# Four product blocks by token halves ahead of a norm, three behind it, and split weights in the common ring

## The chip, the cores and the metric

The kernel runs on one core of a Trainium2 chip. The metric is the device time of one execution in microseconds (us). The median of three runs of the kernel before is 2490.06 us (2487.38 to 2491.95).

## What is computed

Two models one after the other on a sequence of 512 tokens of width 1024, all in float32. The first is one layer with three branches (a forgetting attention, a complex diagonal state-space model, an attention on a memory of 256 rows) and a last norm; the second is two layers (a full attention and three dilated ones) whose norms are shifted and scaled by a projection of a condition c. What the change touches are the products with weights and the norms between them, cut here to:

```python
y = x * rsqrt(mean(x * x, -1) + 1e-6) * g          # rms(x, g), in front of every product below
x = x + merged @ w_out; x = rms(x, g_final)         # end of the first model
for l in range(2):                                  # the second model
    h = rms(x, g_mix[l]) * (1 + sc1) + sh1
    parts = split(h @ w_in[l]); ...                 # attentions on parts give "merged"
    x = x + gt1 * (merged @ w_out[l])
    h2 = rms(x, g_mlp[l]) * (1 + sc2) + sh2
    x = x + gt2 * (square(relu(h2 @ w_ff1[l])) @ w_ff2[l])
```

## The kernel before

**Layout.** Activations lie transposed: eight tiles x[0] to x[7] of 128 features by 512 tokens. A block is a PSUM tile of 128 output features by 512 tokens, the sum over eight tiles of the input.

**Products.** A float32 product is made of three products of fp32r numbers: high times high, low times high, high times low (`mm3`, L108 to L110). So a block of depth 8 takes 24 matmuls of 512 columns. Weights are split on the chip: `fetch` loads a strip of 128x1024 (tag wr), `split` makes the high part with a cast on ACT (tag wh, L88) and the low part with a subtract (tag wl, L90), strips alternating between DVE and POOL. wr, wh and wl have three buffers each in a pool of their own, and `get` splits the strip that it hands out and the two behind it. All other tiles of 128x512 come from one ring of NU = 73.

**Norm.** Squares of x are summed over the eight tiles on ACT and DVE into sacc (`sq_acc`, L174, L175). `rstd` sums sacc over partitions on PE (`sumcols`, L181), DVE makes nv (L199), POOL the power nr (L201), PE spreads nr over the partitions (`bcast`, L188). `hi` then makes hu = x times gain times nr on DVE (L551) and the high half h on ACT (L213, or L215 with a shift); `lo` makes the low half l on DVE (L221, L223). In the norm of block 1 the same steps stand at L1069 and around it, with two norms in one.

**Around a norm.** `tail` emits the last two blocks of the product ahead of a norm by halves of 256 tokens: both blocks for the first half, then both for the second. `head` emits the norm (stat is `rstd`, then hi and lo, each by halves) and the first two blocks (HN = 2; three for "u" in block 1) behind it, by halves too: h against wh and wl (L584, L585), then l against wh (L588). This stands at: the start (norm of x, then "u"), the end of block 1 (then "qa" of layer 0), "out" then "f1" in each of the two layers, and the last "f2" of layer 0 (then "qa" of layer 1). The feed-forward runs in four quarters c, each with f1 and f2; every f2 has a tail.

**Query and key stages.** `qk_stages` norms the heads of a q or k block: squares on ACT (L611), their sums on PE (L617), DVE, POOL and DVE again (a value cut in three parts, L258 to L262, into mcq), PE (L268), ACT (qr, L277), PE (L634), DVE (L635), then the copies of `put`. They run as generators, a stage behind each later block (`run_lag`); `flush` runs what is left. `d_proj(1)` is the projection of one group of the dilated attention in `layer`, and a flush stands at its end. mcm is the same kind of value for the merging of heads.

**Order.** Instructions are emitted in program order with priorities; the framework's scheduler then sets each engine's queue by its own estimate of times, so the rows of a queue can differ from the text. `tick` feeds background work (the condition's projection `ada_gen`, on DVE with loads on SP) between blocks; `drain` finishes it.

## Time and profile before

| what | value |
|---|---|
| median of three runs | 2490.06 us (2487.38 to 2491.95) |
| the profiled execution | 2493.03 us, of which its span 2491.2 us |
| PE, DVE, ACT, POOL busy | 94%, 62%, 42%, 34% of the span |
| mean granted TensorE clock | 0.973 |

A row of a timeline shows the start in us, how long it lasted, the engine, the line, the operation, output<-inputs, the tile and a count; in brackets, the idle time of the engine just before and what ended it. Matmuls overlap in the pipeline, so the pace of PE is the distance from one start to the next, not the duration shown. The granted clock is a share of full speed; 1.00 is 2.4 GHz and 0.5 is 1.2 GHz.

### The profile page before, as it was taken

Reading aid. Unit: us, or ns where it says so; the run is one execution under the profiler, and the core shown is the slowest. Engines: PE = TensorE matmul, PEld = TensorE weight load, DVE = VectorE, ACT = ScalarE, POOL = GpSimd, SP = SyncE. Lnnn points to the kernel's source line nnn. Section 1 sums busy time; section 2 is a strip of 40 time slices with the busy share of each in tenths; the row PEclk is TensorE's granted clock in tenths of the full one; section 3 lists DMA queues with packets and bytes.
Section 4 is the critical chain, followed back from the end, with each engine's and each line's share of the span. In section 5 each row is a group of like instructions: output and inputs, shape, how many; then the busy total and the mean of one; then the engine's idle time right before and its main releaser. Section 6 shows DMA issues by size and latency. Waiting matters only on the chain.

```text
span 2491.2 us, 32131 instructions
## 1 busy us (share of the span) xinstructions
PE 2343.6 (94%) x12162; PEld 1956.8 (79%) x12162; DVE 1543.0 (62%) x2394; ACT 1036.4 (42%) x1639; POOL 840.3 (34%) x637
## 2 busy tenths in 40 slices
PE   7998889988999889998999999998999999999999
PEld 6876667877888767787887888887778887888888
DVE  7666776666898787557378674257875646522222
ACT  5435443443323336543434324334465343423432
POOL 2445446544222463126122122216431622212221
PEclk9999889999999899999999999999999999999999
DMA  5211112322775421122136562232211313232232
GB/s 186 90 48 53 51 60 85 119 68 68 251 259 203 136 89 51 34 69 84 60 119 252 192 224 102 93 119 91 66 54 57 93 56 123 77 101 93 93 102 85
DMA packets 105611, 265.29 MB, mean 106 GB/s; under 512 B 13664, under 2 KB 23408, under 8 KB 105456
## 3 DMA queue, kind: packets, MB, share of 16 engines
q1 hardware_dynamic: 104304, 261.47, 31.4%
q8 instruction: 96, 1.57, 0.3%
q10 hardware_dynamic: 1152, 1.77, 0.2%
q14 instruction: 59, 0.48, 0.1%
HBM read 244.69 MB, written 9.44 MB: 102 GB/s over the span
## 4 chain that ended last, share of the span: by engine, by line
PE 47%; DVE 7%; issue 3%; ACT 2%; DMA 2%; POOL 2%; SPq 1%; DVEq 0%; POOLq 0%; ACTq 0%
PE pmm L108 13%; PE pmm L109 13%; PE pmm L110 13%; PE ps L311 3%; DMA adw<-in_wada 1%; PE ppv L400 1%; PE ppv L402 1%; PE ppv L401 1%; POOL wl L90 1%; DMA xs<-xg 1%; DVE unm L336 1%; DVE xs L624 0%; ACT qk L650 0%; DVE adacc L505 0%; DVE rs L430 0%
## 5 line engine op out<-in xcount | busy, mean ns | idle before, releaser
L108 PE MATMUL pmm<-h,wh 128*128 128x512 f32 (+1 forms) x2232 | 853.6, 384 | 14.7 <-DVE gt L1072 4.1
L90 POOL TENSOR_TENSOR wl<-wr,wh 128x1024 fp32r<-128x1024 f32 (+1 forms) x173 | 423.2, 2446 | 1290.7 <-ACT wh L88 1067.1
L110 PE MATMUL pmm<-h,wl 128*128 128x512 f32 (+1 forms) x2232 | 851.6, 382 | 3.4 <-POOL wl L90 2.8
L109 PE MATMUL pmm<-l,wh 128*128 128x512 f32 (+1 forms) x2232 | 853.0, 382 | 0.0
L88 ACT CAST wh<-wr 128x1024 fp32r<-128x1024 f32 (+1 forms) x346 | 358.2, 1036 | 906.9 <-PE pmm L109 705.0
L108 PEld LDWEIGHTS pmm<-h,wh 128*128 128x128 f32 x2232 | 423.5, 190 | 96.6 <-ACT h L213 5.3
L110 PEld LDWEIGHTS pmm<-h,wl 128*128 128x128 f32 x2232 | 423.6, 190 | 81.5 <-POOL wl L90 3.8
L109 PEld LDWEIGHTS pmm<-l,wh 128*128 128x128 f32 x2232 | 423.8, 190 | 75.4 <-DVE l L221 1.3
L90 DVE TENSOR_TENSOR wl<-wr,wh 128x1024 fp32r<-128x1024 f32 (+1 forms) x173 | 225.5, 1303 | 164.9 <-ACT wh L88 161.9
L960 DVE SCALAR_TENSOR_TENSOR x<-pmm,ada,x 128x512 f32<-128x512 f32 (+1 forms) x100 | 64.2, 642 | 214.0 <-PE pmm L110 213.7
L383 DVE TENSOR_TENSOR pl<-pe,ph 128x512 fp32r<-128x512 f32 (+4 forms) x168 | 121.1, 731 | 117.9 <-ACT ph L381 107.2
L311 PE MATMUL ps<-qk,qk 128*128 128x512 f32 (+4 forms) x416 | 143.9, 380 | 21.8 <-POOL qk L671 9.1
L505 DVE SCALAR_TENSOR_TENSOR adacc<-adw,cact,adacc 128x512 f32<-128x512 f32 x168 | 156.2, 939 | 3.2 <-DMA adw<-in_wada 0.2
L221 DVE TENSOR_TENSOR l<-r,h 128x512 fp32r<-128x512 f32 x64 | 59.3, 928 | 121.5 <-ACT h L213 121.3
L311 PEld LDWEIGHTS ps<-qk,qk 128*128 128x128 f32 x416 | 81.2, 200 | 43.9 <-POOL qk L671 11.3
L379 ACT ACTIVATE pe<-ps 128x512 f32<-128x512 f32 (+4 forms) x168 | 84.4, 503 | 66.4 <-PE ps L311 48.0
L108 PE MATMUL pmm<-yh,wh 128*128 128x512 f32 (+1 forms) x244 | 93.3, 385 | 4.1 <-ACT yh L1402 2.6
L110 PE MATMUL pmm<-yh,wl 128*128 128x512 f32 (+1 forms) x244 | 92.5, 381 | 0.6 <-POOL wl L90 0.6
L381 ACT CAST ph<-pe 128x512 fp32r<-128x512 f32 (+4 forms) x168 | 88.8, 529 | 8.3 <-POOL y L431 2.1
L109 PE MATMUL pmm<-yl,wh 128*128 128x512 f32 (+1 forms) x244 | 92.2, 379 | 0.0
L402 PE MATMUL ppv<-pl,v 128*128 128x512 f32 (+2 forms) x216 | 78.0, 361 | 14.2 <-DVE pl L383 14.1
L336 DVE TENSOR_REDUCE unm<-ps 128x1 f32<-128x512 f32 (+2 forms) x112 | 64.7, 596 | 31.3 <-PE ps L311 30.8
(366 smaller groups left out, 3895.2 us busy)
## 6 DMA issues: line engine op xcount, KB each, us to landing
wr<-in_w SPq DMA_DIRECT2D x324, 512.0 KB
adw<-in_wada SPq DMA_DIRECT2D x192, 256.0 KB
xs<-xg SPq DMA_DIRECT2D x136, 64.0 KB
wr<-in_w SPq DMA_DIRECT2D x22, 384.0 KB
xd<-x SPq DMA_DIRECT2D x16, 256.0 KB
x<-xd SPq DMA_DIRECT2D x16, 256.0 KB
x<-in_x SPq DMA_DIRECT2D x16, 128.0 KB
x<-in_x SPq DMA_DIRECT2D x8, 256.0 KB
```

Source lines behind the costliest of these rows:

```text
L88: self.nc.scalar.copy(h[:, 0:n], r[:, 0:n])
L90: eng.tensor_tensor(out=l[:, 0:n], in0=r[:, 0:n], in1=f32(h)[:, 0:n], op=ALU.subtract)
L108: mm(out, wh, ah, start=start, stop=False)
L109: mm(out, wh, al, start=False, stop=False)
L110: mm(out, wl, ah, start=False, stop=stop)
L311: mm(outs[i] if len(r.shape) == 2 else outs[i].rearrange("p (r i) -> p r i", r=r.shape[1]), w, r, start=first and i == 0, stop=last and i ...
L336: nc.vector.tensor_reduce(out=nm, in_=pts[0], axis=AX.X, op=ALU.max, negate=True)
L379: nc.scalar.activation(out=e[:, w], in_=pt[:, w], func=AF.Exp)
L381: nc.scalar.copy(ph[:, w], e[:, w])
L383: nc.vector.tensor_tensor(out=pl[:, w], in0=e[:, w], in1=f32(ph)[:, w], op=ALU.subtract)
L402: mm(self.cut(pv, c), vh, lo, start=False, stop=z)
L505: nc.vector.scalar_tensor_tensor(out=acc, in0=w, scalar=cc, in1=acc, op0=ALU.mult, op1=ALU.add)
```

## The change

1. **Splits.** A strip is split in pieces of 512 columns. The two or more wh and wl tiles come from the common ring, which grows from 73 to 85; the pool of weights keeps wr alone. A cast no longer waits for one of three wh buffers; a dependency that only the scheduler sees puts it behind the last matmul emitted so far.
2. **Tails.** Ahead of a norm the tail has four blocks (NT = 4; the fourth in another PSUM bank, tag "s") in place of two. The norm is built before the tail; stat(0) is emitted behind the first block of the second half, hi(0) behind the second one. f2 of the first three quarters has no tail any more: eight full blocks. The last f2 of the kernel keeps two blocks.
3. **Heads.** Three blocks (HN = 3) in place of two, except "u", which has two in place of three. Where a tail began the norm, the head leaves stat(0) and hi(0) out.
4. **Order of the rest.** The condition's projection is drained before the tail in block 1 and in the last f2 of layer 0.
5. **hu.** Both halves of a norm share eight hu tiles; before, each half had eight of its own.

The diff, cut:

```diff
-    NU = 73
-    NW = 3, 3, 3
+    AFTER = mybir.DependencyInfo(mybir.DependencyClass.NoSync, mybir.DependencyReason.SCHED_ONLY)
+    NU = 85
+    NW = 3, 3
@@ split
-        h = self.t(self.wp, [128, 1024], F32R, "wh", self.NW[1])
-        l = self.t(self.wp, [128, 1024], F32R, "wl", self.NW[2])
-        self.nc.scalar.copy(h[:, 0:n], r[:, 0:n])
         eng = self.nc.gpsimd if i % self.WP == self.WP - 1 else self.nc.vector
-        eng.tensor_tensor(out=l[:, 0:n], in0=r[:, 0:n], in1=f32(h)[:, 0:n], op=ALU.subtract)
-        self.hl[i] = (h, l)
+        self.hl[i] = []
+        for c in range(0, n, T):
+            m = min(T, n - c)
+            h, l = self.u(F32R, "wh"), self.u(F32R, "wl")
+            ins = self.nc.scalar.copy(h[:, 0:m], r[:, c:c + m])
+            if self.pe is not None:
+                self.tc.add_manual_dep(ins.ins, self.pe, self.AFTER, reason="weights")
+            eng.tensor_tensor(out=l[:, 0:m], in0=r[:, c:c + m], in1=f32(h)[:, 0:m], op=ALU.subtract)
+            self.hl[i].append((h, l))
@@ mm3 (fm, tm and head keep the name of their last matmul in the same way)
-        mm(out, wl, ah, start=False, stop=stop)
+        self.pe = mm(out, wl, ah, start=False, stop=stop).ins.name
@@ norm, hi(hf), and the same in the norm of block 1
-                u = self.u(name="hu")[:, 0:256]
+                if hf == 0:
+                    us.append(self.u(name="hu"))
+                u = self.half(us[j], hf)
@@ head
-    def head(self, names, h, posts, norm, view, byw=False):
+    def head(self, names, h, posts, norm, view, byw=False, begun=False):
...
-        stat(0)
-        hi(0)
+        if not begun:
+            stat(0)
+            hi(0)
@@ tail
-    def tail(self, name, act, posts):
+    def tail(self, name, act, posts, norm=None):
         ws = [self.get(name, 8) for _ in posts]
-        pms = [self.p("mm") for _ in posts]
+        pms = [self.p("mm" if i < 3 else "s") for i in range(len(posts))]
...
                 self.tick(2.6)
+                if norm is not None and hf == 1 and i < 2:
+                    norm[i](0)
@@ constants
-    HN = 2
+    HN = 3
+    NT = 4
@@ layer, out (block 1's out alike, with the background drained ahead of the tail)
-        for s in range(3):
-            for f in self.strip(f"out{l}", xm, 8, [res(2 * s + b, 16, True) for b in range(2)]):
-                f()
-        self.tail(f"out{l}", xm, [res(6 + b, 16, True) for b in range(2)])
+        nt = self.NT
+        for f in self.strip(f"out{l}", xm, 8, [res(j, 16, True) for j in range(8 - nt)]):
+            f()
         h = self.new_h()
         norm = self.norm(x, mod[:, 8:16], ada[:, 24:32], h)
+        self.tail(f"out{l}", xm, [res(j, 16, True) for j in range(8 - nt, 8)], norm)
@@ layer, feed-forward
-            for s in range(3):
-                for f in self.strip(f"f2{l}", F, 8, [res(2 * s + b, 40, sq) for b in range(2)]):
-                    f()
-            self.tail(f"f2{l}", F, [res(6 + b, 40, sq) for b in range(2)])
+            nt = 0 if c < 3 else 2 if out is not None else self.NT
+            for f in self.strip(f"f2{l}", F, 8, [res(j, 40, sq) for j in range(8 - nt)]):
+                f()
+            if c == 3:
+                norm = None
+                if out is None:
+                    del h
+                    self.drain(g)
+                    h = self.new_h()
+                    self.mod[l + 1] = self.mod_cols(l + 1)
+                    norm = self.norm(x, self.mod[l + 1][:, 0:8], self.ada[l + 1][:, 0:8], h)
+                self.tail(f"f2{l}", F, [res(j, 40, sq) for j in range(8 - nt, 8)], norm)
@@ block 1, behind the first norm
-        self.head(["u"] * 3, h, [upost(j) for j in range(3)],
+        self.head(["u"] * 2, h, [upost(j) for j in range(2)],
                   norm, self.half, True)
```

How it moves the queues, at three places. Lines of the changed kernel are nine higher for the same statement (L117 to L119 are L108 to L110, L190 is L181, L197 is L188, L593 is L584, L93 is L88, L662 is L650, L222 is L213).

PE, between "out" and "f1" of layer 0, before (xh and xl are the input of out, ps the small sums, ppv and pmm the two blocks of the head):

```order
L109 MATMUL pmm_11667<-xl_11426,wh_11620 128x256
L110 MATMUL pmm_11667<-xh_11425,wl_11621 128x256
L181 MATMUL ps_11798<-c_2_67,sacc_11477 128x1 x2
L188 MATMUL ps_11805<-c_2_67,nr_11803 128x128 x2
L181 MATMUL ps_11844<-c_2_67,sacc_11477 128x1 x2
L584 MATMUL ppv_11796<-h_11780,wh_11654 128x256
L585 MATMUL ppv_11796<-h_11780,wl_11655 128x256
```

PE there now, around the sums of the first half:

```order
L119 MATMUL pmm_12335<-xh_12028,wl_12240 128x256
L117 MATMUL pmm_12335<-xh_12041,wh_12239 128x256
L190 MATMUL ps_12478<-c_2_67,sacc_12159 128x1 x2
L118 MATMUL pmm_12335<-xl_12042,wh_12239 128x256
L119 MATMUL pmm_12335<-xh_12041,wl_12240 128x256
```

and around the spreading of nr:

```order
L117 MATMUL pmm_12336<-xh_12064,wh_12298 128x256
L118 MATMUL pmm_12336<-xl_12065,wh_12298 128x256
L197 MATMUL ps_12485<-c_2_67,nr_12483 128x128 x2
L119 MATMUL pmm_12336<-xh_12064,wl_12299 128x256
L117 MATMUL pmm_12336<-xh_12077,wh_12298 128x256
```

Before, sums, spreading and the first product of the head stand directly behind one another, behind the last product of out. Now 28 matmuls of 256 columns of out stand between the sums and the spreading, and 34 between the spreading and the first product of the head. The other norm of layer 0's end and the one of layer 1 have the same pattern; at the end of block 1 there are nine matmuls between sums and spreading.

ACT, at the start, before (sq are the squares of x, h the high half of the first norm):

```order
L174 ACTIVATE sq_167<-x_114 128x256
L88 CAST wh_235<-wr_131 128x1024
L174 ACTIVATE sq_170<-x_115 128x256
L174 ACTIVATE sq_173<-x_116 128x256
L174 ACTIVATE sq_176<-x_117 128x256
L174 ACTIVATE sq_179<-x_118 128x256
L88 CAST wh_241<-wr_239 128x1024
L213 CAST h_182<-hu_211 128x256
```

and now:

```order
L222 CAST h_188<-hu_228 128x256
L222 CAST h_186<-hu_222 128x256
L222 CAST h_187<-hu_225 128x256
L222 CAST h_188<-hu_228 128x256
L222 CAST h_189<-hu_231 128x256
L93 CAST wh_234<-wr_131 128x512
L222 CAST h_189<-hu_231 128x256
L93 CAST wh_238<-wr_131 128x512
L93 CAST wh_244<-wr_242 128x512
```

The first cast of a weight stood between the squares of x; now it stands behind 15 of the 16 casts of h. On PE, sums and spreading of both halves now stand ahead of the first product.

ACT, at the flush at the end of `d_proj(1)` of layer 0, before (qk are the copies of `put`, qr the rows of the last stage, wh_10623 and wh_10803 weights of the products that follow):

```order
L277 CAST qr_10476<-ps_10471 128x512
L277 CAST qr_10499<-ps_10494 128x512
L650 CAST qk_10488<-xg_10334 64x512
L650 CAST qk_10491<-xg_10334 64x512
L88 CAST wh_10623<-wr_10347 128x1024
L88 CAST wh_10803<-wr_10555 128x1024
L650 CAST qk_10504<-xg_10414 64x512
L650 CAST qk_10510<-xg_10414 64x512
```

and now:

```order
L662 CAST qk_11114<-xg_10956 64x512
L662 CAST qk_11117<-xg_10956 64x512
L286 CAST qr_11125<-ps_11120 128x512
L662 CAST qk_11130<-xg_11040 64x512
L662 CAST qk_11136<-xg_11040 64x512
L93 CAST wh_11177<-wr_10827 128x512
L93 CAST wh_11181<-wr_10827 128x512
```

The casts of the next weights now stand behind all copies of the flush (wh_11177 and wh_11181 are the second strip of the products of v, pmm_11267 and pmm_11388). On PE, 23 products of 256 columns are left between the last sums of squares (L617) and the last spreading of mcq (L268) of this flush; the products with wh_11177 come behind the first scores (L311).

## Rows read from the trace of the kernel before

**Rows 1.** The page, busy time and instructions of each engine.

```profile
PE 2343.6 (94%) x12162; PEld 1956.8 (79%) x12162; DVE 1543.0 (62%) x2394; ACT 1036.4 (42%) x1639; POOL 840.3 (34%) x637
```

**Rows 2.** Waits of PE: who ended them; us in total, times, longest.

```profile
PE ps L268 <- DVE mcq L262: 20.2, 9, 3.8
...
PE ps L188 <- POOL nr L201: 10.4, 5, 2.7
```

**Rows 3.** PE by stretches: length, busy (instructions), granted clock, DMA share, GB/s.

```profile
1290.00:1320.00 30.00, 26.78 (x181) 0.89 0.11 36
...
2122.00:2152.00 30.00, 26.79 (x179) 0.89 0.11 36
800.00:842.00 42.00, 36.13 (x235) 0.84 0.26 85
...
1320.00:1340.00 20.00, 17.48 (x77) 1.00 0.89 322
```

**Rows 4.** Timeline of PE, from out to f1 of layer 0.

```profile
1294.94 0.50 PE L181 MATMUL ps<-c,sacc 128*128 128x1 f32 x4
1298.19 1.23 PE L188 MATMUL ps<-c,nr 128*128 128x128 f32 x4 [2.74 <-POOL nr L201]
...
1300.53 0.58 PE L584 MATMUL ppv<-h,wh 128*128 128x256 f32 x1 [0.47 <-ACT h L215]
...
1304.41 0.28 PE L585 MATMUL pmm<-h,wl 128*128 128x256 f32 x1
1304.53 0.28 PE L584 MATMUL ppv<-h,wh 128*128 128x256 f32 x1
```

**Rows 5.** Timeline of DVE, POOL and ACT in the same place.

```profile
1293.31 2.39 POOL L90 TENSOR_TENSOR wl<-wr,wh 128x1024 fp32r<-128x1024 f32 x1 [11.78 <-ACT wh L88]
1293.58 2.40 DVE L175 TENSOR_TENSOR sacc<-sacc,sq 128x256 f32<-128x256 f32 x1 [0.83 <-ACT sq L174]
...
1296.52 1.61 POOL L201 TENSOR_TENSOR nr<-nv,mhalf 128x2 f32<-128x2 f32 x1 [0.82 <-DVE nv L199]
...
1297.50 0.41 DVE L175 TENSOR_TENSOR sacc<-sacc,sq 128x256 f32<-128x256 f32 x1
...
1299.45 0.88 DVE L551 SCALAR_TENSOR_TENSOR hu<-x,modc,ps 128x256 f32<-128x256 f32 x2 [1.54 <-PE ps L188]
1299.97 3.35 ACT L215 ACTIVATE h<-hu,ada 128x256 fp32r<-128x256 f32 x8 [3.14 <-DVE hu L551]
```

**Rows 6.** Timeline of PE, from block 1 to layer 0.

```profile
812.05 0.95 PE L181 MATMUL ps<-c,sacc 128*128 128x1 f32 x8
817.42 1.19 PE L188 MATMUL ps<-c,nr 128*128 128x128 f32 x4 [4.42 <-DVE nr L1069]
```

**Rows 7.** Timeline of ACT and PE at the start.

```profile
12.56 1.04 ACT L88 CAST wh<-wr 128x1024 fp32r<-128x1024 f32 x1 [1.90 <-DMA wr<-in_w]
...
16.70 0.58 PE L584 MATMUL ppv<-h,wh 128*128 128x256 f32 x1 [3.11 <-ACT h L213]
...
19.11 1.01 PE L181 MATMUL ps<-c,sacc 128*128 128x1 f32 x4 [1.41 <-DVE sacc L175]
```

**Rows 8.** Timeline of PE: a merging of heads, then the flush, in layer 0.

```profile
929.89 0.61 PE L268 MATMUL ps<-c,mcm 128*128 128x128 bf16 x4 [3.39 <-DVE mcq L262]
...
1146.15 1.05 PE L617 MATMUL ps<-c,sq 128*128 128x2 f32 x8 [0.44 <-ACT sq L611]
...
1156.57 0.40 PE L268 MATMUL ps<-c,mcq 128*128 128x128 bf16 x4 [3.77 <-DVE mcq L262]
...
1164.85 0.39 PE L634 MATMUL ps<-qr,c 128*128 128x512 bf16 x1
```

**Rows 9.** Casts of ACT by line and form: ns shortest/median/longest, first and last start.

```profile
L88 ACT CAST wh<-wr x346: 817/1052/1082, 12.6 to 2470.9; 128x1024 fp32r<-128x1024 f32 x162, 128x768 fp32r<-128x768 f32 x11
...
L213 ACT CAST h<-r x64: 619/621/626, 1321.5 to 2446.0; 128x512 fp32r<-128x512 f32 x64
L213 ACT CAST h<-hu x16: 399/406/408, 16.2 to 29.5; 128x256 fp32r<-128x256 f32 x16
```

More of the change, by code (lines that the diff above doesn't have):

```diff
@@ L101, in get @@
         self.iw += 1
-        n = self.strips[i][1].shape[-1]
-        return tuple(t[:, 0:n].rearrange("p (k c) -> p k c", k=kb) for t in self.hl.pop(i))
+        c = self.strips[i][1].shape[-1] // kb
+        per = T // c
+        hl = self.hl.pop(i)
+        self.hl[i] = None
+        return [tuple(t[:, c * (k % per):c * (k % per) + c] for t in hl[k // per]) for k in range(kb)]
     def mm3(self, out, wh, wl, ah, al, start=True, stop=True):
@@ L109, in mm3 @@
         mm(out, wh, al, start=False, stop=False)
-        mm(out, wl, ah, start=False, stop=stop)
+        self.pe = mm(out, wl, ah, start=False, stop=stop).ins.name
     def fm(self, out, w, c0, act, kb):
-        (wh, wl), (ah, al) = w, act
-        for k in range(kb):
-            self.mm3(out, wh[:, k, c0:c0 + 128], wl[:, k, c0:c0 + 128], ah[k], al[k], k == 0, k == kb - 1)
+        ah, al = act
+        for k, (wh, wl) in enumerate(w):
+            self.mm3(out, wh[:, c0:c0 + 128], wl[:, c0:c0 + 128], ah[k], al[k], k == 0, k == kb - 1)
     def tm(self, out, ws, act, tok, cols=slice(0, 256)):
@@ L121, in tm @@
         mm = self.nc.tensor.matmul
-        ks = [(wh[:, k, cols], wl[:, k, cols]) for wh, wl in ws for k in range(wh.shape[1])]
+        ks = [(wh[:, cols], wl[:, cols]) for w in ws for wh, wl in w]
         for k, (wh, wl) in enumerate(ks):
@@ L125, in tm @@
             mm(out, ah[k][:, tok], wl, start=False, stop=False)
-            mm(out, al[k][:, tok], wh, start=False, stop=k == len(ks) - 1)
+            self.pe = mm(out, al[k][:, tok], wh, start=False, stop=k == len(ks) - 1).ins.name
     def tick(self, us=5.2):
@@ L541, in norm @@
         sacc = self.sums["sacc"]
-        pr, hu = {}, {}
+        pr, hu, us = {}, {}, []
         def stat(hf):
@@ L582, in head @@
                 for k in range(8):
[L583 to L585 removed]
+                    for w, o in g:
+                        mm(o, w[k][0], ah[k], start=k == 0, stop=False)
+                        mm(o, w[k][1], ah[k], start=False, stop=False)
                 for k in range(8):
[L587 to L588 removed]
+                    for w, o in g:
+                        self.pe = mm(o, w[k][0], al[k], start=False, stop=k == 7).ins.name
         for pm, post in zip(pms, posts):
@@ L779, in tm_items, with layer @@
         return [lambda g=g: f(g) for g in range(4 // per)]
-    def layer(self, l, norm, view, x, out=None):
+    def layer(self, l, h, norm, view, x, out=None):
         nc = self.nc
-        ada = self.ada[l]
-        mod = self.mod_cols(l)
+        ada, mod = self.ada[l], self.mod[l]
         xd = self.xdram[l]
-        h = self.new_h()
         Y = {}
@@ L804, in layer @@
         ps = [post(cq, self.CA, self.SA, True, ("a", b)) for b in range(4)]
-        self.head([f"qa{l}"] * self.HN, h, ps[0:self.HN], norm(h, mod, ada), view)
+        self.head([f"qa{l}"] * self.HN, h, ps[0:self.HN], norm, view, begun=True)
         for j in range(8):
@@ L991, in layer @@
                 n = self.HN
-                self.head([f"f1{l}"] * n, h, [relu2] * n, norm, self.half)
+                self.head([f"f1{l}"] * n, h, [relu2] * n, norm, self.half, begun=True)
             for f in self.strip(f"f1{l}", h, 8, [relu2] * (8 - n)):
@@ L1495, in block1 @@
         self.load16()
-        self.merge(self.strip("u", h, 8, [upost(j) for j in range(3, 6)]), [])
+        self.merge(self.strip("u", h, 8, [upost(j) for j in range(2, 6)]), [])
         merged = []
@@ L1719, in res @@
             return f
-        for s in range(3):
-            for f in self.strip("out", ms, 8, [res(2 * s), res(2 * s + 1)]):
-                f()
-        self.tail("out", ms, [res(6), res(7)])
+        nt = self.NT
+        for f in self.strip("out", ms, 8, [res(j) for j in range(8 - nt)]):
+            f()
+        while self.bg:
+            self.drain(self.bg[0])
         xo = [self.u(name="x") for _ in range(8)]
@@ L1751, in hi @@
                 for j in range(8):
-                    u = self.u(name="hu")[:, 0:256]
+                    if hf == 0:
+                        us.append(self.u(name="hu"))
+                    u = self.half(us[j], hf)
                     self.stt(u, self.half(x[j], hf), self.gfm[:, j:j + 1], p2[hf], ALU.mult, ALU.mult)
@@ L1766, in s5_out @@
         self.gfm = self.t(self.base, [128, 8], F32, "gfm")
-        return xo, norm
+        h = self.new_h()
+        self.mod[0] = self.mod_cols(0)
+        norm = norm(h, self.mod[0], self.ada[0])
+        self.tail("out", ms, [res(j) for j in range(8 - nt, 8)], norm)
+        return xo, h, norm
 PERM = np.arange(T).reshape(128, 4).T.reshape(-1)
@@ L1995, in run @@
     def run(self, out):
-        x, norm = self.block1()
-        while self.bg:
-            self.drain(self.bg[0])
+        self.mod = {}
+        x, h, norm = self.block1()
         self.load2()
-        x = self.layer(0, norm, self.halfp, x)
-        self.layer(1, self.plain(x), self.half, x, out)
+        x, h, norm = self.layer(0, h, norm, self.halfp, x)
+        self.layer(1, h, norm, self.half, x, out)
 INS = ["x", "mem", "c32", "c16", "rope", "trow", "mb0", "cols", "w1024", "w768", "wada", "wfl", "s5p", "s5bc", "bfg"]
```

16 lines of the change are left out of this document (4 added, 12 removed).

## The prediction

> **What bounds the kernel.** I read the page first. PE is busy 94% of the span of 2491.2 us, DVE 62%, ACT 42%, POOL 34% [rows 1]: only what makes PE idle, or slow, can be won. That is some 148 us of idle time and what is lost at the lower clock (mean 0.973). The waits of PE show it in many small pieces: the query and key stages (mcq, 20.2 us in 9 waits) and the norms (nr, 10.4 us in 5) lead [rows 2]. So I went to the places that the change touches.
>
> The stretch of a norm comes three times in alike form, from out to f1 of both layers and from f2 of layer 0 to layer 1. In 30 us around the first and the last PE is busy 26.78 and 26.79 us, with a granted clock of 0.89 [rows 3]: 3.2 us idle, and 0.11 of 30 us is 3.3 us of lost clock, that is 6.6 us at 1.2 GHz. The timeline says why [rows 4]: the sums start at 1294.94, the spreading waits 2.74 us for nr and starts at 1298.19, the first product waits another 0.47 and starts at 1300.53. The low clock follows that idle time; idle time in smaller pieces need not bring it, as the stretch at 1320 us shows, with 2.5 us idle in 20 us and a clock of 1.00 [rows 3]. On the other engines [rows 5] the reader sees the links: an addition to sacc takes 2.40 us where the next takes 0.41, since it runs beside a weight subtract of POOL that takes 2.39; POOL's power of two columns takes 1.61; two steps of hu take 0.88, and eight casts of h 3.35.
>
> **The change, part by part.** The sum is made against the profiled execution, 2493.03 us, which is 2.97 above the median of the runs, 2490.06; the forecast is given against the median.
>
> *Three alike norms.* The lag between sums and spreading was 3.25 us (1294.94 to 1298.19) [rows 4]. Now 28 matmuls of 256 columns stand there. At the full clock these come 0.12 us apart (1304.41, 1304.53) [rows 4], so the cover is 3.4 us. From the spreading to the first product it was 2.34 us (1298.19 to 1300.53); now 34 matmuls, 4.1 us, stand there. Both are covered, the first barely. If so the idle 3.2 us goes; and of the 6.6 us at 1.2 GHz the part that was not idle, 3.4 us, did half its work and loses 1.7 us, which is also won. What is late next: the head's third block needs a weight whose low half now stands behind nv of the second half on DVE, and the sums of the second half have only 15 matmuls (1.8 us) before their spreading, against a lag of 3.25. That leaves 1.0 to 1.5 us of idle time. 3.2 + 1.7 − 1.2 is 3.7; the small sums and spreadings, which ran at the low clock and now run among products, give some 0.3 more. I take 4.0 each, **12.0** together. Bounds: 1 each if the remaining idle time still brings the low clock, 5.2 each if nothing is late.
>
> *From block 1 to layer 0.* PE is busy 36.13 of 42 us, clock 0.84 [rows 3]. The spreading waits 4.42 us, at a distance of 5.37 from the sums [rows 6]. Only nine matmuls (1.1 us) now stand between; some 3.3 us of that wait stay and may bring the low clock again, while what comes behind is covered. Bounds: 0 and 5. I take the middle, **2.5**.
>
> *The start.* The first cast of a weight began at 12.56, and the first product at 16.70 [rows 7]. Products then came at the pace of h, and after the sums at 19.11 (1.01 us) without a break, so the start was worth being full from about 20.1. Now the first cast stands behind 15 casts of h. The first of these started at 16.2 and one takes 0.41 [rows 9]; they follow hu, of which one takes 0.44 (0.88 for two) [rows 5]. The fifteenth ends at about 16.2 + 14 × 0.44 + 0.41 = 22.8, and half a strip's cast of 0.62 ends at 23.4 [rows 9]. The loss is 23.4 − 20.1 = **3.3**. Bounds: 1.8 (the sums of the second half are out of the way by then) and 5 (the low half on DVE comes later too).
>
> *Splits.* A strip's cast was 1.05 us; two pieces take 2 × 0.62 = 1.24 [rows 9]: 0.19 more for each of 346 strips, 66 us at most on ACT, which is busy 1036 of 2491 us [rows 1]. ACT's own work hides it; if ACT were the last in a stage, the price would be there in full. I put it at nothing, but for the two places named (start, flush).
>
> *Shapes of products.* The full blocks of three quarters' f2, the tails of four and the heads of three change which products run with 256 columns and which with 512: 24 more of 512 and 48 fewer of 256. 48 of 256 at 0.12 are 5.8 us, and 24 of 512 are about the same, a little less by what each matmul costs beside its columns; I take **0.3** won (bounds 0 and 0.6).
>
> *Attention.* Casts no longer wait for one of three buffers, and the order of PE shifts. A wait for mcm of 3.39 us [rows 8], alike in both layers, now has 6.6 us of products ahead of them in the order in place of 0.7: 6.8 us to be won at most. The flush that follows gives some back. Between its last sums (1146.15) and its last stage (1164.85) lay 18.7 us, with 0.44 and 3.77 us of idle time [rows 8]. Now only 23 products of 256 columns (2.8 us) stand between the last sums and the last spreading, and the next weights' casts come behind all copies: two of 0.62. I take half of the first, 3.4 won, and two such casts late in each layer, 2.4 lost: **1.0** won. Bounds: 6.8 won, 21.8 lost (the rival below).
>
> The sum: −12.0 − 2.5 + 3.3 − 0.3 − 1.0 = **−12.5**; the profiled execution would be 2480.5 us, the median 2477.6, so **2478**. The terms' own uncertainty gives 2472 to 2484.
>
> **The rivals.** *More is won.* The addition to sacc took 2.40 us beside a subtract of POOL [rows 5]; half-length subtracts would hold it up half as long, some 1.2 us, and there are other such meetings on the way to the norms and in the flush. Six places of 1.2 us are 7 us: 2471. For it speaks that row; against it that most steps of DVE are not waited for. The Trainium skill's page "SBUF — State Buffer", section "Who interferes with whom", says that a DVE instruction with two SBUF inputs contends with a GpSimd instruction that reads SBUF, and that the loser is fully blocked for the whole instruction. By that rule, halving the subtract halves the block, and the time would be this rival's; the trace agrees as far as the pair of 2.39 and 2.40 goes.
>
> *No change.* The three norms give about 1 us each, since the spreading of the second half comes too early and what idle time is left still brings the low clock, block 1's end gives nothing with its nine matmuls, and the start takes 3.3: −3 + 3.3 − 0.3 − 1 = −1, 2489. That would be a change that doesn't do what it says. For it speaks the barely covered lag (3.4 against 3.25); against it that the second wait is fully covered.
>
> *Slower: the flush.* The chain from the last sums to the last stage took 18.7 us, mostly beside products [rows 8]. If it takes as long with 2.8 us of products and some 1 us of small ones beside it, PE is idle 15 us in place of 4.2 in each of two layers: +10.8 twice, 21.6, against the forecast's 2.4 or so. The time is 2478 + 22 = 2500. It decides from about 6 us of added idle time per layer, where all else that is won is gone. For it speaks that all of the chain's copies are on DVE, ACT and POOL, whatever PE does. Against it: part of the 18.7 us was queueing behind subtracts of weights and copies that have moved away, and the waits for mcq before were no longer than 3.8 [rows 2].
>
> **How the numbers follow.** A measurement of this kernel can tell about 0.2% (5 us) from no change. Chances: forecast 0.46, more won 0.13, no change 0.23, slower 0.18. Faster by over 0.2% (under 2485) is the first two, 0.59, and a little of the third, so 0.60; no change is the rest of the third, 0.22; slower (above 2495) 0.18. The range reaches below to 2464 (more won, with the norms' upper bound of 5.2 each) and above to 2500, which leaves out half of the slower case and little else. The forecast's own range is 2472 to 2484.
>
> **What would show it.** Right: in the three norms, PE's waits for nr gone or under 1 us and the granted clock of such a stretch at 0.97 or more in place of 0.89; the first product at about 23 us at the start; waits for mcm near nothing; the flush within 2 us of before. Wrong: a clock still below 0.93 around the norms, or a wait of PE at the end of the flush of over 8 us, or new waits of PE for wl or wh of over 10 us in sum, which would mean that the splits come too late.

## The result and the profile after

The changed kernel takes 2459.40 us (median of 4 runs, 2458.20 to 2460.29) against 2490.52 us (2487.38 to 2491.95): a ratio of 0.9876, 95% interval 0.9859 to 0.9894, so 31 us faster. The forecast was 12.5 us faster, 2478 (2464 to 2500).

The page of the changed kernel answers to [rows 1] and, for the casts, to the idle time that the three buffers made (its last two rows; idle time and what ended most of it stand at the end of a row):

```profile
span 2457.6 us, 33152 instructions
...
PE 2322.2 (94%) x12138; PEld 1938.8 (79%) x12138; DVE 1538.6 (63%) x2573; ACT 1064.0 (43%) x1995; POOL 887.5 (36%) x810
...
L93 ACT CAST wh<-wr 128x512 fp32r<-128x512 f32 (+1 forms) x692 | 385.1, 610 | 136.8 <-DMA wr<-in_w 118.8
L96 DVE TENSOR_TENSOR wl<-wr,wh 128x512 fp32r<-128x512 f32 x346 | 278.8, 836 | 30.3 <-ACT wh L93 26.9
```

and the row of the kernel before for the same casts:

```profile
L88 ACT CAST wh<-wr 128x1024 fp32r<-128x1024 f32 (+1 forms) x346 | 358.2, 1036 | 906.9 <-PE pmm L109 705.0
```

PE's idle time fell from 147.6 to 135.4 us (span less busy), 12 us; its busy time fell by 21.4 us at equal work, since the mean granted clock rose from 0.973 to 0.981. Casts waited for PE before (a buffer of wh to be done with); now they wait for their load.

**A table by stage.** To see where the time goes, I laid the starts of PE's instructions of two traces beside each other at equal work: each matmul counts as what it takes at the full clock (0.227 us for 512 columns, 0.1185 for 256), and a stage is a stretch of that sum. What stands there is how much a kernel falls behind the kernel before over a stage, in us, negative where it is faster (one profiled execution of each kernel; the last stage, under 1.5 us everywhere, is only in the sum). The stages end at 61, 131, 384, 781, 864, 1283, 1342, 1405, 1642, 1696, 2113 and 2171 us of the kernel before: the start; two stretches of block 1; its attention and state-space part ("attn 1" is 131 to 384 us); the passage to layer 0; layer 0's attention; its norm; the first of its f1; the rest of the feed-forward; the norm of layer 1; and so on. A stage is good to about 2 us. The sums are up to 7 us more favourable than the medians of the runs, as the profiled execution of the kernel before, 2493.03 us, was one of its longer ones: cast_halves has −8.2 in the table and −1 by its runs.

```
kernel            start  -131  attn1  rest1  to l0  attn l0  norm   f1  ff  norm  attn l1  norm   all
changed             9.7  -5.0  -11.8    4.5    3.3    -16.0  -5.9 -2.3   0  -4.7     -0.3  -4.8 -33.7
halves_in_pool     -1.0  -0.4  -10.6    2.1   -2.3      0.1  -2.0 -0.5  -1  -3.1     -0.7  -2.1 -21.6
splits_only        12.1  -4.9   -4.9    3.8   -1.1    -11.3   1.1 -2.4  -1   3.1     -1.5   2.7  -4.7
no_overlap          9.1  -4.9  -10.1    5.0   -5.8    -10.7   0.2 -2.3  -1   2.9     -0.2   1.7 -16.5
early_split        15.3  -4.9   -5.6    6.9    2.9    -15.6  -6.2 -2.4  -1  -4.6     -0.6  -4.8 -21.0
mid_split           4.0  -5.2   -6.0    4.5    3.4    -14.9  -6.0 -2.4   0  -4.7      1.1  -4.7 -31.0
pool_halves        -1.4  -1.3  -19.4   -1.7   -1.9     -1.2  -2.8 -1.5   0  -1.8      0.6  -1.9 -34.6
dve_halves         -0.6  -0.4   -8.0    1.6    2.7     -0.9   0.0  0.6   0  -0.6     -2.4  -0.9  -8.8
cast_halves         0.6  -1.1  -12.0    2.5    1.6     -0.6   0.5  0.4   0   0.0     -0.1  -0.1  -8.2
norms_only         -0.9   0.9  -17.0   -0.1    3.5     -6.1   3.5 -2.3  -1   6.4      5.2   6.3  -2.0
before_pool_256    -1.4  -1.8  -16.6   -4.8   -4.8      1.1  -1.1 -1.2  -1  -2.4      4.5  -2.5 -32.1
pool_halves_nt3    -2.0  -0.8  -15.2   -2.6   -3.9     -2.7   1.2 -2.6  -1  -0.2     -0.5   0.9 -30.6
after_pool_256      9.6  -3.6  -11.1    3.6    2.5    -14.4  -6.1 -2.6  -1  -4.6      1.1  -4.8 -32.2
before_u2          -1.0   0.7  -18.9    0.5    1.4     -2.1   0.1 -0.5   0  -1.3     -2.2   0.1 -22.7
before_swapped      2.0  -5.7  -15.1   -5.2    4.2     -3.8  -0.5 -0.3   0  -0.3      2.1  -0.6 -23.1
after_swapped       9.1  -1.1  -11.6    0.1    1.1     -7.4  -4.0 -2.3   0  -3.4      1.3  -3.5 -22.6
no_after           10.3  -5.2  -10.6    4.4    5.3    -15.2  -6.0 -2.6   0  -4.7      0.2  -4.6 -29.4
hybrid             -0.4  -2.2  -14.8   -4.2   -3.4     10.0  -6.2 -2.3   0  -4.7     14.5  -4.8 -19.1
after_nu73          9.6  -5.0  -12.0    8.6   -1.4     13.2  -6.0 -2.3   0  -4.7     13.5  -4.5   8.1
```

The reader is to see four things in the first row: the three norms (−15.4 together), a start that loses 9.7, and two stretches of attention, −11.8 and −16.0, that the prediction did not have (it had 1.0 us won in all attention).

**The norms.** PE's timeline between out and f1 of layer 0 in the changed kernel answers to [rows 4]:

```profile
1274.22 0.50 PE L190 MATMUL ps<-c,sacc 128*128 128x1 f32 x4
1278.02 0.60 PE L197 MATMUL ps<-c,nr 128*128 128x128 f32 x4
...
1289.44 0.71 PE L197 MATMUL ps<-c,nr 128*128 128x128 f32 x4 [0.55 <-POOL nr L210]
1290.96 0.39 PE L597 MATMUL ppv<-l,wh 128*128 128x256 f32 x1 [0.81 <-DVE l L232]
1294.67 0.39 PE L593 MATMUL ppv<-h,wh 128*128 128x256 f32 x1 [0.32 <-ACT h L224]
```

and the stretches of the three norms, by windows (length, busy, granted clock, DMA share, GB/s), to [rows 3]; the fourth is the passage from block 1:

```profile
1270.00:1300.00 30.00, 28.32 (x230) 1.00 0.42 143
1636.00:1666.00 30.00, 28.34 (x222) 1.00 0.24 82
2094.00:2124.00 30.00, 28.34 (x222) 1.00 0.16 54
790.00:832.00 42.00, 35.39 (x260) 0.96 0.36 126
```

The spreading of the first half waits for nothing, 1.7 us of idle time are left in three small pieces, and the clock is 1.00 where it was 0.89. What the lower clock had cost there is seen in the kernel before, in the part of the first norm's stretch at 1.2 GHz (a granted clock of 0.50):

```profile
1297.15:1303.97 6.82, 5.31 (x24) 0.50 0.39 139
```

PE was busy for 5.3 of these 6.8 us, and for 6.1 in each of the other two norms.

**The start.** PE's timeline answers to [rows 7]; behind it stand the low halves of h on DVE:

```profile
23.12 0.58 PE L593 MATMUL ppv<-h,wh 128*128 128x256 f32 x1 [4.75 <-ACT wh L93]
33.99 0.38 PE L597 MATMUL ppv<-l,wh 128*128 128x256 f32 x1 [4.01 <-DVE l L230]
```

```profile
33.52 5.45 DVE L230 TENSOR_TENSOR l<-hu,h 128x256 fp32r<-128x256 f32 x16
```

**Layer 0's attention**, PE's timeline in the kernel before, with a wait at each step of scores and softmax:

```profile
1002.35 0.50 PE L311 MATMUL ps<-qk,qk 128*128 128x512 f32 x1 [1.27 <-ACT pe L379]
...
1006.09 0.44 PE L311 MATMUL ps<-qk,qk 128*128 128x128 f32 x2 [1.36 <-DVE ut L340]
...
1007.87 0.80 PE L402 MATMUL ppv<-pl,v 128*128 128x512 f32 x1 [1.21 <-DVE pl L383]
```

and in the changed kernel in the same part of the work, where products with weights (L117, L118) stand between the steps of the attention (L320) and nothing waits (two such waits, 1.28 and 0.68 us, are left a little ahead, at 990 and 994 us):

```profile
1002.99 0.39 PE L117 MATMUL pmm<-h,wh 128*128 128x512 f32 x1
1003.22 0.39 PE L118 MATMUL pmm<-l,wh 128*128 128x512 f32 x1
...
1003.90 0.39 PE L320 MATMUL ps<-qk,qk 128*128 128x512 f32 x1
...
1004.35 0.39 PE L118 MATMUL pmm<-l,wh 128*128 128x512 f32 x1
```

By windows, the kernel before has there

```profile
1000.00:1020.00 20.00, 16.15 (x60) 0.83 0.00 1
```

and the changed one

```profile
1000.00:1020.00 20.00, 20.00 (x95) 1.00 0.23 79
```

**The flush and the passage.** In the changed kernel PE waits for mcq at the end of the flush in layer 0 (to [rows 8]; 6.40 us in layer 1) and once more at the end of the passage from block 1:

```profile
858.54 0.61 PE L277 MATMUL ps<-c,mcq 128*128 128x128 bf16 x4 [5.48 <-DVE mcq L271]
...
1142.99 0.61 PE L277 MATMUL ps<-c,mcq 128*128 128x128 bf16 x4 [6.42 <-DVE mcq L271]
```

The wait for mcm of [rows 8] is gone in both layers:

```profile
924.61 0.40 PE L277 MATMUL ps<-c,mcm 128*128 128x128 bf16 x4
```

### The profile page after: what moved, and what is told of

Same layout as the page of the kernel before. It is cut to its first block, busy times and chain, and to the rows that moved or that the text cites. A ratio compares the mean times of both kernels' runs of the same rounds, so it can differ in the third digit from the quotient of the medians.

```text
span 2457.6 us, 33152 instructions
## 1 busy us (share of the span) xinstructions
PE 2322.2 (94%) x12138; PEld 1938.8 (79%) x12138; DVE 1538.6 (63%) x2573; ACT 1064.0 (43%) x1995; POOL 887.5 (36%) x810
## 4 chain that ended last, share of the span: by engine, by line
PE 63%; DVE 11%; issue 4%; ACT 3%; POOL 2%; DMA 1%; SPq 1%; DVEq 0%; POOLq 0%; ACTq 0%
PE pmm L117 17%; PE pmm L118 17%; PE pmm L119 17%; PE ps L320 3%; DVE wl L96 1%; DVE adacc L514 1%; DMA xs<-xg 1%; PE ppv L411 1%; PE ppv L410 1%; PE ppv L409 1%; DVE l L232 1%; PE pmm L134 1%; PE pmm L135 1%; PE pmm L133 1%; DVE xs L636 1%
## 5 line engine op out<-in xcount | busy, mean ns | idle before, releaser
L96 POOL TENSOR_TENSOR wl<-wr,wh 128x512 fp32r<-128x512 f32 x346 | 480.8, 1409 | 1122.6 <-ACT wh L93 968.0
L117 PE MATMUL pmm<-h,wh 128*128 128x512 f32 (+1 forms) x2112 | 824.1, 391 | 5.7 <-ACT wh L93 3.2
L119 PE MATMUL pmm<-h,wl 128*128 128x512 f32 (+1 forms) x2112 | 821.2, 389 | 2.1 <-POOL wl L96 1.8
L118 PE MATMUL pmm<-l,wh 128*128 128x512 f32 (+1 forms) x2112 | 819.5, 388 | 0.0
L119 PEld LDWEIGHTS pmm<-h,wl 128*128 128x128 f32 x2112 | 399.1, 189 | 85.7 <-POOL wl L96 4.3
L117 PEld LDWEIGHTS pmm<-h,wh 128*128 128x128 f32 x2112 | 399.4, 189 | 84.7 <-ACT wh L93 4.7
L118 PEld LDWEIGHTS pmm<-l,wh 128*128 128x128 f32 x2112 | 399.6, 189 | 77.3 <-DVE l L230 0.4
L93 ACT CAST wh<-wr 128x512 fp32r<-128x512 f32 (+1 forms) x692 | 385.1, 610 | 136.8 <-DMA wr<-in_w 118.8
L96 DVE TENSOR_TENSOR wl<-wr,wh 128x512 fp32r<-128x512 f32 x346 | 278.8, 836 | 30.3 <-ACT wh L93 26.9
L320 PE MATMUL ps<-qk,qk 128*128 128x512 f32 (+4 forms) x416 | 142.9, 381 | 24.6 <-POOL qk L683 7.4
L994 ACT ACTIVATE r<-pmm 128x512 f32<-128x512 f32 x62 | 37.1, 598 | 257.1 <-PE pmm L119 257.1
L320 PEld LDWEIGHTS ps<-qk,qk 128*128 128x128 f32 x416 | 81.0, 199 | 51.7 <-POOL qk L683 13.3
L117 PE MATMUL pmm<-yh,wh 128*128 128x512 f32 (+1 forms) x244 | 91.2, 377 | 5.8 <-ACT yh L1419 3.7
L632 POOL TENSOR_TENSOR qv<-qv,mhalf 128x8 f32<-128x8 f32 x34 | 62.9, 1852 | 86.6 <-DVE qv L631 83.1
L119 PE MATMUL pmm<-yh,wl 128*128 128x512 f32 (+1 forms) x244 | 90.7, 373 | 1.7 <-DVE wl L96 0.9
L118 PE MATMUL pmm<-yl,wh 128*128 128x512 f32 (+1 forms) x244 | 90.6, 372 | 0.3 <-DVE yl L1089 0.3
```

What stands on the lines that cost most here:

```text
L93: ins = self.nc.scalar.copy(h[:, 0:m], r[:, c:c + m])
L96: eng.tensor_tensor(out=l[:, 0:m], in0=r[:, c:c + m], in1=f32(h)[:, 0:m], op=ALU.subtract)
L117: mm(out, wh, ah, start=start, stop=False)
L118: mm(out, wh, al, start=False, stop=False)
L119: self.pe = mm(out, wl, ah, start=False, stop=stop).ins.name
L320: mm(outs[i] if len(r.shape) == 2 else outs[i].rearrange("p (r i) -> p r i", r=r.shape[1]), w, r, start=first and i == 0, stop=last and i ...
```

## The experiments

All ratios are to the kernel before, run on the same chip.

**1. Only the pieces.** `halves_in_pool`, in split of the kernel before:

```diff
-        self.nc.scalar.copy(h[:, 0:n], r[:, 0:n])
...
-        eng.tensor_tensor(out=l[:, 0:n], in0=r[:, 0:n], in1=f32(h)[:, 0:n], op=ALU.subtract)
+        for c in range(0, n, T):
+            s = slice(c, min(c + T, n))
+            self.nc.scalar.copy(h[:, s], r[:, s])
+            eng.tensor_tensor(out=l[:, s], in0=r[:, s], in1=f32(h)[:, s], op=ALU.subtract)
```

> The kernel before with one edit: a strip is cast and subtracted in two pieces of 512 columns, into the same three 128x1024 buffers as before. Theory A (short subtracts: DVE and POOL hold each other up half as long) expects most of the 18 us that the prediction missed here: 2472 to 2480. Theory B (the order: casts that wait for no buffer let the scheduler lay the queues of the attentions differently) and theory C (the blocks around the norms) expect no change: 2487 to 2493.

2472.1 us, 0.9928 (0.9905 to 0.9952). This looked like theory A; the runs below say why it need not be, for the most part. It also shows that pieces alone win nothing in layer 0's attention (+0.1).

**2. Only the splits of the change.** `splits_only`:

```diff
-    HN = 3
-    NT = 4
+    HN = 2
+    NT = 2
...
-                if norm is not None and hf == 1 and i < 2:
+                if False:
```

with begun=False, a head of three for u, and nt = 2 in every f2.

> The changed kernel with its splits, ring and shared hu, but tails of two blocks, heads of two (three for u), every f2 with a tail, and no norm begun inside a tail. Theory A expects what halves_in_pool gives, plus the late start of some 9 us: within 10 us of it. Theory B expects the attentions' gain of about 15 us in the two stretches 60 to 280 us and 840 to 1040 us here: 2470 to 2478. Theory C expects no gain at all but the start's loss: 2490 to 2500.

2488.9 us, 1.0009 (0.9998 to 1.0020). None of the three, though by the number alone theory C's 2490 is near: by stage it wins 11.3 in layer 0's attention and loses 12.1 at the start and 7 at the norms, where its heads wait for h, wh and l (0.5 to 1.3 us each).

**3. No norm inside the tail.** `no_overlap`: only `if False:` and begun=False of the edit above.

> The changed kernel, but the norm is emitted behind the tail (stat(0) and hi(0) in the head, as before); four and three blocks stay. If the cover by the tail's products is what wins at the norms (prediction: 4 us at each of three, 2.5 at the fourth), 12 to 20 us are lost: 2472 to 2480. If the blocks alone or the splits win it, under 5 us: 2459 to 2464.

2478.2 us, 0.9957 (0.9943 to 0.9970): some 19 us are lost, as expected if the cover wins. It does so at the three norms, which come to +4.8 without it and to −15.4 with it. At the fourth place, from block 1 to layer 0, it doesn't: that passage and the attention of layer 0 behind it come to −12.7 together with the cover and to −16.5 without it.

**4. An early first split.** `early_split` (self.split(0) with high priority ahead of the squares) and **8.** `mid_split`, with its edit:

```diff
+                if hf == 1 and j == 3:
+                    self.split(0)
+        self.split(1)
```

> The changed kernel, but the first strip is split ahead of the first squares, with high priority. The start lies 9.6 us behind the kernel before at 61 us in the trace. If that loss is the late first cast and is carried to the end, the time falls to 2449 to 2454. If what follows makes it good anyway (the attention of block 1 bounded by other engines), 2456 to 2460.

> The changed kernel, with its first strip split after twelve of the sixteen squares of x and its second after all of them, so that on ACT both stand ahead of h and none waits long for its load. The changed kernel loses 9.7 us at the start; early_split lost 15.3 there because the squares stood behind a cast that waited for its load until 11.86 us. If the late cast is the start's loss, PE is 7 to 10 us ahead of the changed kernel at 61 us. If that is carried to the end: 2449 to 2453. If the attention of block 1 swallows it, 2455 to 2460.

2471.7 us, 0.9931 (0.9911 to 0.9951), and 2462.1 us, 0.9889 (0.9873 to 0.9906). The first is a miss: its cast stood in front of the squares until the load came at 11.86 us. The second wins 5.7 of the 9.7 us at the start (7 to 10 were expected) and loses as much by 384 us (−6.0 in place of −11.8). A start that is made good is not carried to the end there.

**5 to 7. One engine's pieces at a time**, on the kernel before. `pool_halves`, and the same on DVE or on ACT alone:

```diff
+        w = T if eng is self.nc.gpsimd else n
+        for c in range(0, n, w):
...
```

> The kernel before, with the low halves in two pieces of 512 columns on POOL alone (casts and DVE's subtracts whole). halves_in_pool, all in halves, measured 2472. Theory A (a long subtract on POOL holds DVE's short instructions up) expects most of that gain here: 2472 to 2480. Theory D (what counts is that a whole subtract or cast stands in the way in DVE's and ACT's own queue) expects under a third of it: 2484 to 2490.

> The kernel before, with the low halves in two pieces on DVE alone (casts and POOL's subtracts whole). Theory A expects little, as POOL's 2.4 us stay: 2483 to 2490. Theory D expects about half of the 16 us: 2477 to 2483.

> The kernel before, with the casts on ACT in two pieces, the subtracts whole on both engines. Theories A and D on DVE expect no gain, 2486 to 2494 (66 us more of ACT time, hidden). If ACT's queue is what counts, 2477 to 2483. If each new order of the queues moves the time by itself, whatever it shortens, 5 us or more in either direction.

2459.5 us, 0.9884 (0.9868 to 0.9900); 2484.4 us, 0.9981 (0.9971 to 0.9991); 2487.4 us, 0.9996 (0.9981 to 1.0010). POOL's pieces alone win about as much as the whole change, more than either theory expected of them. But by stage 19.4 us of it lie in block 1's attention, and little in the layers' attentions. The others have 8 and 12 there, too, but their runs win only 5 and 1 us, so of those two gains it is not shown how much is more than the one profiled execution.

**9. The change's blocks on the old splits.** `norms_only` (old split and get, ring of 73, three buffers, tails of four begun as in the change), and **10.** `pool_halves_nt3` (the same with NT = 3 and POOL in halves).

> The changed kernel's tails of four blocks, heads of three, norm begun in the tail, shared hu and full f2, on the splits of the kernel before (whole strips, three buffers of wh and wl, ring of 73). In the order the sums, the spreading and the first product stand behind one another again at all three alike norms: with three buffers the fourth strip's split waits for the first to be done, so the tail's halves can't interleave. If the ring is needed for the cover, the norms cost as before and more, by a head of three: 2488 to 2500. If the blocks win by themselves: 2465 to 2475.

> As norms_only, but tails of three blocks (which three buffers hold) and POOL's subtracts in halves. In the order 38 rows stand between sums and spreading at the three norms, one between spreading and head. Theory A (POOL's pieces) and the cover of the first wait add up: pool_halves' 2459.5 less some 3 us at each of three norms: 2449 to 2454. If the two overlap, or the second wait grows by what the first loses: 2457 to 2462.

2495.2 us, 1.0016 (1.0003 to 1.0029), and 2463.1 us, 0.9888 (0.9869 to 0.9908). The blocks need the ring: with three buffers the norms lose 3.5, 6.4 and 6.3 us. And block 1's attention wins 17.0 us with whole subtracts on POOL, so a gain of that size there needs no shorter ones; it has the change's head of two blocks of u (run 13 below). A cover of the first wait alone (nt3) wins nothing on top of POOL's pieces.

**11, 12. POOL in pieces of 256**, on both kernels.

> The kernel before with POOL's subtracts in four pieces of 256 columns. Theory A in its strict form (a shorter piece holds DVE for a shorter time) expects pool_halves' 2459.5 or better: 2450 to 2462. If pool_halves owes its gain to one lucky order of the queues in block 1, this one scatters back: 2470 to 2490.

> The changed kernel with POOL's subtracts in pieces of 256 columns, four to a strip. Theory A expects another gain, smaller than the first: 2445 to 2456. If what is left in the changed kernel is not POOL's length: 2456 to 2464.

2460.3 us, 0.9875 (0.9856 to 0.9894); 2460.6 us, 0.9879 (0.9863 to 0.9894): no more on either than with pieces of 512.

**13 to 15. Other orders.** `before_u2` (a head of two blocks of u, which is also a part of the change); `before_swapped` and `after_swapped`:

```diff
-        eng = self.nc.gpsimd if i % self.WP == self.WP - 1 else self.nc.vector
+        eng = self.nc.gpsimd if i % self.WP == 0 else self.nc.vector
```

> The kernel before with one edit: the first head takes two blocks of u in place of three. norms_only, whose splits are whole as before, gained 17 us by 280 us and kept 20 of them to the end of block 1, as much as pool_halves there. If block 1's gain is not the length of POOL's pieces but an order of the queues that the kernel before has and most others don't, this gains 10 to 18 us in block 1 and nothing behind it: 2472 to 2481. If the gain needs the shorter pieces: 2486 to 2494.

> The kernel before with the strips' engines swapped (POOL subtracts the first, DVE the second, and so on): the same work, sizes and buffers. It shows how far an order alone moves the time: within 4 us of 2490 if orders matter little, 2470 to 2485 or over 2495 if they matter much.

> The changed kernel with the same swap. In the layers behind block 1 the change gained 30 us in the trace: 16 by the norm's cover, 10 by its splits, 4 by the blocks. If those are its mechanisms, the layers stay within 5 us of that, whatever block 1 does; if the splits' 10 us are luck of the order, they move by as much.

2472.1 us, 0.9933 (0.9917 to 0.9948); 2473.6 us, 0.9936 (0.9919 to 0.9953); 2468.0 us, 0.9912 (0.9890 to 0.9935). The first changes, beside the order, one block of 512 columns for two halves of 256 (24 more products of 512, 48 fewer of 256, which the prediction put at 0.3 us for the whole change); the second changes only which engine subtracts which strip. By their ratios they win 16 to 17 us, nearly all in block 1: by 781 us before_u2 has −18.7 and before_swapped −24.0. The whole change, which has the head of before_u2 in it, has −2.6 there. Under the swap the changed kernel keeps −10.9 of −15.4 at its norms and half of layer 0's attention (−7.4). Behind block 1's passage it wins 19 us in place of 34, so the layers moved by more than the 5 us expected of the change's mechanisms: an order is worth some 5 us at the norms and 9 in layer 0's attention, too.

**16. Without the order-only dependency.** `no_after` (`if False:` in place of `if self.pe is not None:`).

> The changed kernel without the dependency that puts each cast behind the last emitted matmul. If that dependency is what keeps DVE behind in the first 120 us (it has done 78 us of work there, the kernel before 85), block 1 gains about 10 us: 2447 to 2453. If it is what wins in the layers (casts out of the way of the attentions), they lose 5 to 10: 2464 to 2470. If it does neither: 2457 to 2462.

2462.2 us, 0.9891 (0.9876 to 0.9906): it does neither, within what the measurement can tell.

**17. A hybrid**, and **18. a ring of 73** (`NU = 73` in the changed kernel). The hybrid, in split:

```diff
+        if self.strips[i][0][-1] not in "01":
+            h = self.t(self.wp, [128, 1024], F32R, "wh", 3)
+            l = self.t(self.wp, [128, 1024], F32R, "wl", 3)
...
```

> Block 1 with the old splits (three buffers of 1024, POOL in pieces of 256, head of three, tail of two with the norm begun in it), the two layers with the change's splits from the ring (73 tiles, as there is no room for 85 beside the buffers), its tails of four and heads of three. By stages, against the kernel before: block 1 as in before_pool_256 (-25 us, no late start), the layers as in the changed kernel (-30 us). If the stages stand for themselves: 2433 to 2442. If a ring of 73 undoes what the ring won in the attention of layer 0: 2446 to 2454. If an order's luck in block 1 doesn't hold once more: 2452 to 2460.

> The changed kernel with a ring of 73 tiles in place of 85, so weights and activations together have the room that activations alone had before. If the depth of the ring is what lets products run ahead in the attention of layer 0 (-16 us there), about 10 us of that go: 2466 to 2472. If it is enough that pieces need no buffers of their own: 2457 to 2463.

2473.7 us, 0.9936 (0.9924 to 0.9948), and 2499.4 us, 1.0039 (1.0026 to 1.0052). The ring of 73 costs the changed kernel 40 us, four times what was expected, and the table says where: 29 us in layer 0's attention (+13.2 for −16.0) and 14 in layer 1's; the norms stand (−6.0, −4.7, −4.5). The waits of the kernel before in the softmax are back in its timeline of PE, almost to the number:

```profile
1004.96 0.50 PE L320 MATMUL ps<-qk,qk 128*128 128x512 f32 x1 [1.28 <-ACT pe L388]
...
1008.70 0.44 PE L320 MATMUL ps<-qk,qk 128*128 128x128 f32 x2 [1.36 <-DVE unm L350]
...
1010.44 0.80 PE L411 MATMUL ppv<-pl,v 128*128 128x512 f32 x1 [1.18 <-DVE pl L392]
```

Within layer 0's attention, by the same reckoning, the difference lies between 960 and 1100 us of the kernel before: −13.7 with 85 tiles, +6.6 with 73 (and +7.0 in the hybrid). Between 925 and 940 us, where the wait for mcm stood, it is −7.3 with 85 and −7.5 with 73, so that gain does not hang on the size of the ring.

In the hybrid the stages of block 1 and of the norms add up as expected (−25.0 to layer 0, −15.7 at the norms); what undid it is the same ring, +10.0 and +14.5 in the attentions; the time lies above all three of its expected ranges. No version beat the changed kernel by more than the measurement can tell. For a hybrid with 85 tiles there is no room beside the old buffers.

## Why the prediction was wrong

The sign was right and the size was not: the time lies 5 us below the range. By its own steps:

- **Three alike norms, −12.0.** Right in mechanism, a little small: −5.9, −4.7, −4.8, together −15.4. The lag of 3.25 us was covered; the next lateness was the second half's nr, l and h (0.55, 0.81 and 0.32 us, 1.7 together, where 1.0 to 1.5 was expected). What was under-priced is the lower clock. The working took the idle 3.2 us to lie inside the 6.6 us at 1.2 GHz, which left 3.4 us of slow work and 1.7 to win; but PE was busy 5.3 to 6.1 us of that time, so 2.7 to 3.1 were to be won, and the lower clock went altogether. no_overlap shows the cover as the cause. That a shorter subtract of POOL also helps the norms is shown on the old order: 2 to 3 us at each with pool_halves, halves_in_pool and before_pool_256 (but one of 1.1), within 1 us of nothing with dve_halves and cast_halves.
- **From block 1 to layer 0, −2.5.** Missed: +3.3. The wait for nr fell from 4.42 to 1.06 us, more than nine matmuls' worth, and the clock rose (0.84 to 0.96). But PE's idle time in the 42 us went up, from 5.9 to 6.6 us, in new waits for h, l and wl, and the wait of 5.48 us for mcq stands behind it in the same stage, where 0.50 us had stood.
- **The start, +3.3.** The first product came at 23.12 us, forecast 23.4; but the low halves, which I had not followed, came to DVE only at 33.52, behind other work, and PE waited 4.01 us more. The loss was 9.7. DVE's queue had to be read on to l, not only to the first wl. splits_only, which has the old head of three blocks of u, loses 12.1 us there, so it is the splits that bring it.
- **Splits at nothing and shapes, −0.3.** ACT's longer casts were hidden: ACT rose from 1036 to 1064 us, and cast_halves shows no difference. But the splits come late, and a sign that the prediction had named for being wrong came true: PE's waits for wh and wl are 21.4 us in sum, where they were 4.7. The longest groups (us in total, times, longest):

```profile
PE pmm L117 <- ACT wh L93: 5.1, 6, 1.9
...
PE ppv L593 <- ACT wh L93: 4.8, 1, 4.8
...
PE pmm L134 <- DVE wl L96: 3.7, 3, 2.5
```

All but 1.7 us of the 21.4 lie ahead of 830 us, 4.8 of them in the first product of the start. What the others cost block 1 was not tried by itself. The quarters' full f2 is within 1 us of nothing in all kernels.
- **Attention, −1.0, bounds −6.8 and +21.8.** This is the step that failed. It priced two places of the layers, a wait for mcm and the flush, and put all other attention at nothing. Together these two came out at about nothing, near its 1.0. The wait for mcm is gone in both layers, and the lead grows by 7 us in each at that place, about half of which is given back next. The flush did get worse: a wait of 6.42 us and smaller ones in place of 3.77, some 3 to 4 us in each layer, as the rival for slower has it, at a third of its price. What it left out are −16.0 in layer 0 and −7.3 in block 1 between 131 and 781 us. Most of layer 0's part needs the ring of 85 tiles, shown by after_nu73 (+13.2). splits_only, with this ring and none of the blocks, has −11.3; halves_in_pool, with pieces but separate buffers, has +0.1. I read NU = 85 as room for what had been buffers and gave it no term. It is that room, the 73 tiles and the six buffers of two tiles each; what is new is that products with weights and tiles of the attention share it, so that, by the timelines above, products stand in the gaps of the softmax. The order has its share, too: with the swap half of the gain is left. In block 1, by the table, an order alone does more than the change: before_swapped, whose edit the change doesn't have, wins 15.1 us in its attention. before_u2, whose edit is part of the change and was priced only by its shapes, wins 18.9. What of the change's −11.8 there is this head and what the other parts add or take away was not tried on the changed kernel.
- **The rivals.** "More is won" by shorter subtracts: right in sign, wrong in place. Most of what looked like it (pool_halves, −29 us) lies in block 1, where an order alone wins as much; what is clear of it are the norms.

Open is what exactly makes the order of the kernel before slow in block 1. Open, too, is part of what POOL's pieces win: pool_halves and before_pool_256 end 9 to 12 us ahead of before_u2 and before_swapped in the table (12 to 15 by their ratios), some 5 us of it at the norms; for the rest, nothing here tells a shorter hold on DVE from one more order.

## What to carry to other kernels

Where a scheduler orders the queues, compare the order over each whole stage in which an engine waits, not only at the places that an edit names, and give a larger common pool a term of its own: tiles are what lets independent work into a stage's gaps. Before a gain is put down to an edit, run one or two edits that change the order and nothing else; here those alone moved the time by 16 to 17 us, about half of the change's gain. A table by stage at equal work of the bounding engine separates parts that totals hide: the changed kernel and pool_halves both stand at 2459 us and won much of their 30 us in different places. One trace per kernel is not enough for a few us, though: lay its sum beside the median of the runs.

## What the runs showed of the hardware

The lower clock did not go by the idle time's sum (a stretch's granted clock is the mean over its time at 2.4 GHz, 1.00, and at 1.2 GHz, 0.50). In pool_halves the three norms have

```profile
1260.00:1290.00 30.00, 27.95 (x201) 0.94 0.16 53
1628.00:1658.00 30.00, 28.18 (x186) 0.89 0.15 53
2088.00:2118.00 30.00, 28.22 (x190) 0.89 0.12 37
```

In the last two, 1.8 us are idle and the clock is 0.89, as with 3.2 us in the kernel before; in the first, 2.0 us and 0.94. The changed kernel has 1.7 us idle in such a stretch and 1.00, and the kernel before 2.5 us and 1.00 at 1320 us [rows 3]. In the norms of pool_halves sums, waits and spreading stand directly behind one another; in the changed kernel and at 1320 us the waits stand among products with weights. What of this decides wasn't tried by itself.

In pool_halves an addition to sacc beside a POOL subtract of half length (two of them in the row of POOL) took 1.30 us, where 2.40 had stood beside the whole one [rows 5]:

```profile
1266.58 1.30 DVE L178 TENSOR_TENSOR sacc<-sacc,sq 128x256 f32<-128x256 f32 x1 [0.84 <-ACT sq L177]
```

```profile
1266.31 2.71 POOL L93 TENSOR_TENSOR wl<-wr,wh 128x512 fp32r<-128x512 f32 x2 [11.19 <-ACT wh L88]
```

This agrees with the Trainium skill's page "SBUF — State Buffer", section "Who interferes with whom", by which the one that comes second is blocked for the whole instruction of the other: half the instruction, half the block.
